# The input projection in a fixed order of instructions, with later places for convolution tiles

## The chip, the cores and the metric

The kernel runs on one core of one Trainium2 chip. The metric is the device time of one execution in microseconds. Three runs of the kernel before took 1119.25, 1124.59 and 1125.08 us, with a median of 1124.59.

The core has TensorE (PE; PEld is its weight load), VectorE (DVE), ScalarE (ACT), GpSimd (POOL) and SyncE (SP), which here issues nearly all DMAs. Each engine works through its own instructions in order and waits on semaphores for the others.

## The reference

The model is a diffusion backbone of two layers, in float32, on 512 latent tokens and 256 context tokens of width 1024. Cut to what the change touches:

```
m = silu(c) @ w_ada + b_ada                # shifts, scales, gates of a layer
h = rms_norm(x + pos, g); h = h * (1 + scale) + shift      # context the same
z = h @ w_in                               # split into u (512), v (512), gate (512)
y_a = S5(u)                                # 32 groups of 16 channels, 64 states, both directions
y_a = gelu(y_a + d_skip * u); y_a = y_a * sigmoid(y_a @ w_glu)
v = v * sigmoid(gate)
v = silu(layer_norm(depthwise_conv31(v)))  # conv branch
x = x + gate_1 * (concat(y_a, v) @ w_out)
```

The context tokens only feed the states that S5 starts from. Behind the mixer come a squared-ReLU MLP of width 4096, the second layer (a pooling mixer and another MLP) and a last RMS norm.

## The kernel before

Activations are held with the features on the 128 partitions: 1024 features are eight blocks of 128, and the tokens run along the free axis. Most matmuls are done in float32 split in two parts, high and low, with three products: high by high, low by high, high by low (`mm3`, `split`).

**Input projection of u.** It runs over the eight feature blocks d (L863 to L887 below). For a block, `u_load` issues the DMAs of the code weights (`wah`, `wraw`) and of the projection weights (`wu`). `u_ada` multiplies the code vector with these weights: 16 small matmuls into `ps_ada`, a copy by ScalarE into `ada`, two selecting matmuls with `sel`, and two small operations of VectorE, which give the block's scale and shift `ab`. `norm_x` adds the position embedding to all eight blocks, squares them on ScalarE (`sx`, `sq`), sums the squares over blocks on VectorE, and sums over partitions on TensorE, by matmuls against a column of ones (`ps_ms`). `bcast_rsqrt` takes the reciprocal root, sets it on a diagonal `dg`, and spreads it to all partitions by one matmul (`ps_r`). `w_step` splits the projection weights into `wuh` and `wul`. `x_step` makes the modulated block (`tn` on VectorE, its high part `nh` on ScalarE, its low part `nl` on VectorE) and runs 12 matmuls of 512 columns into four accumulators `ux`. `c_step` does the same for a context block with 6 matmuls into `uc`. A table, `CORD`, says in which turn each context block is done.

**Discretisation.** `discretise` (called in turn 2), `phases` and `discretise_b` (turn 3) compute the constants of the state-space part from its parameters: many small operations on VectorE, and 32 copies on ScalarE into the tables `PG` and `PO`.

**State-space part.** The 32 groups are done in eight steps of four. `step_params` prepares a step's tables (`gg`, `O`, `hx`, `Bb`; `sd` and from it, by DMA, `Kt`), and `step_main` runs it: `ps_v` from the transposed inputs `U`, the scan on VectorE (`rr`, `tv`), and the output `ps_y`.

**Work handed out between the steps.** The strings `FILL0` (behind the first three `step_params`) and `FILL` (behind each step) say what other work is emitted there: `v` a tile of values and gates (48 matmuls into `ps_vg`), `c` a depthwise convolution of a quarter of the channels (16 DMAs `cvt<-vpad`, 32 matmuls into `ps_cv`), `a` some tiles of the remaining code weights, `y` and `z` the activations of half the outputs, `n` the layer norm of the conv branch, `h` the second load of x, `k` and `g` the gate of y_a, `w` the output projection.

**Order.** The program is written in one stream, and a scheduler that keeps a model of the times sets the order on each engine when the kernel is built. What the strings and `CORD` give is the order in which work is emitted, which the scheduler may change.

Of the kernel before, what the change touches and what calls it, by code (L numbers as in the profile page):

```python
# [8 lines left out]
F32 = mybir.dt.float32  # L9
# [88 lines left out]
def body(tc, I, out, dbg=None):  # L98
    nc = tc.nc
    V, S, G, PE = nc.vector, nc.scalar, nc.gpsimd, nc.tensor  # L100
    dma = nc.sync.dma_start

    def dq(t, i):
        return S.dma_start if t[i % len(t)] == "S" else dma

# [6 lines left out]
    def add(e, o, a, b):  # L112
        e.tensor_tensor(o, a, b, op=OP.add)
# [38 lines left out]
    with tc.tile_pool(name="persist", bufs=1) as P, tc.tile_pool(name="ps", bufs=1, space=PSUM) as PS:  # L152
# [152 lines left out]
        def mixer0(P0):  # L305
# [26 lines left out]
            x0 = htile("x0", [128, KT, L])  # L332
            load_x(x0, "xK")
            ctx = P0.tile([128, KT, LC], F32, name="ctx", tag="A")
# [19 lines left out]
            def ada_pe(srcs, ld, tag="n"):  # L354
                n = len(srcs)
                ws = [l(src) for l, src in zip(ld, srcs)]

                def go():
                    ps = bank("ps_ada", tag)
                    for i, w in enumerate(ws):  # L360
                        for kt in (0, 2, 4, 6, 1, 3, 5, 7):
                            j = kt // 2
                            PE.matmul(ps[32 * j:32 * j + 32, i * 128:i * 128 + 128], S2[:, kt, :], w[kt],  # L363
                                      start=kt % 2 == 0, stop=kt % 2 == 1, tile_position=(0, 32 * j))
                    a = P0.tile([128, 256], F32, name="ada", tag="ada", bufs=1)[:, :n * 128]
                    copy(S, a, ps[:, 0:n * 128])
                    p2 = ps[:, 256:256 + 2 * n]
                    for i in range(n):
                        PE.matmul(p2[:, 2 * i:2 * i + 2], a[:, i * 128:i * 128 + 128], sel[:, 0:2], start=True, stop=True)
                    return p2.rearrange("p (m v) -> p m v", v=2)  # L370
                return go
# [9 lines left out]

            sx = P0.tile([128, 2, L], F32, name="sx", tag="ysb")
            Rs = [small(L), small(LC)]

            def norm_x():
                for d in range(KT):
                    add_pos_k(E("pos", d), x0, d)
                    if d < 2:
                        S.activation(sx[:, d], x0[:, d], AF.Square)
                    else:  # L390
                        q = w4("sq", "cv")
                        S.activation(q, x0[:, d], AF.Square)
                        add(V, sx[:, d % 2], sx[:, d % 2], q)
                add(V, sx[:, 0], sx[:, 0], sx[:, 1])
                copy(S, Rs[0], bcast_rsqrt([sx[:, 0]], L, D))

            def norm_c():
                qs = []
                for d in range(0, KT, 2):
                    q = w4("sq", "cv")  # L400
                    S.activation(q.rearrange("p (a b) -> p a b", a=2), ctx[:, d:d + 2], AF.Square)
                    if qs:
                        add(V, qs[0], qs[0], q)
                    qs.append(q)
                add(V, qs[0][:, 0:LC], qs[0][:, 0:LC], qs[0][:, LC:2 * LC])
                copy(S, Rs[1], bcast_rsqrt([qs[0][:, 0:LC]], LC, D))

# [3 lines left out]
            ux = [bank("ux", "s"), bank("ux", "s"), u2[:, 0], u2[:, 1]]  # L411
            uc = [bank("uc", "c") for _ in range(2)]
            ab = P0.tile([128, KT, 2, 2], F32, name="ab")
# [3 lines left out]
            def u_load(d):  # L417
                adas[d] = ada_pe([I["wada0"][d, 0], I["wada0"][d, 1]], (ada_half, ada_full))
                wus[d] = w4("wu", WU[d % len(WU)])
                dma(wus[d], I["win_u"][d])  # L420
                if d == 0:
                    dma(ctx, I["ctxT"])
                if d == 2:
# [6 lines left out]

            def u_ada(d):
                p2 = adas[d]()
# [4 lines left out]
            whl = {}  # L437

            def u_mod(src, R, n, d, v, oh, ol, el):
                t = tmp("tn", n)  # L440
                stt(t, src, ab[:, d, 1, v:v + 1], R, OP.mult, OP.mult)
                split_shift(oh, ol, t, ab[:, d, 0, v:v + 1])

# [8 lines left out]
            def w_step(d):  # L452
                if d in (0, 1):
                    w = P0.tile([128, 2, GQ, T + 2, PH], F32R, name="wuhl", tag="O", bufs=2).rearrange("p r q t h -> p (r q t h)")
                    whl[d] = w[:, 0:512], w[:, 512:1024]
                else:
                    whl[d] = w4("wuh", "e", F32R), w4("wul", "e", F32R)
                split(*whl[d], wus[d], S, V)

            def x_step(d):  # L460
                u_mod(x0[:, d], Rs[0], L, d, 0, nh[:, d], nl[:, d], E("ul", d))
                u_mm(nh[:, d], nl[:, d], d, ux)

            def c_step(d):
                c2 = w4("c2", "cv", F32R)
                ch, cl = c2[:, 0:LC], c2[:, LC:2 * LC]
                u_mod(ctx[:, d], Rs[1], LC, d, 1, ch, cl, E("ucl", d))
                u_mm(ch, cl, d, uc)

# [108 lines left out]
            def discretise_b(cfr, cfi):  # L578
# [7 lines left out]

                t = gh(w4("tb", "cv")[:, :512])
                cmul(EC("bb"), Bb[:, :, 0], Bb[:, :, 1], gh(Br_), gh(Bi_), bc(cfr), bc(cfi), t)
# [3 lines left out]

            def phases():
                te = small(NG * NB // 2)
                n, lv = 1, 1
                while n < NB:
# [3 lines left out]
                    n *= 2  # L600
                    lv += 1

            def step_params(st):
# [258 lines left out]

            QS = []  # L863
            u_load(0)
            u_ada(0)
            norm_x()
            u_load(1)
            w_step(0)
            x_step(0)
            u_ada(1)  # L870
            norm_c()
            cf = None
            for d in range(1, KT):
                if d + 1 < KT:
                    u_load(d + 1)
                if 1 < d < KT:
                    u_ada(d)
                w_step(d)
                for i in CORD[d]:
                    c_step(i)  # L880
                if d < KT:
                    x_step(d)
                if d == 2:
                    cf = discretise()
                if d == 3:
                    phases()
                    discretise_b(*cf)  # L887
            Z = P0.tile([96, NG, T, PH], F32, name="Z", tag="A")
# [31 lines left out]
            def ada_rest(m, d):  # L920
                p2 = ada_pe([I["wada0b"][m - 2, d], I["wada0b"][m - 2, d + 1]], (ada_full, ada_full), AT)()
                add(V, mod[:, 0, m, d:d + 2], p2[:, :, 0], bada[:, 0, m * KT + d:m * KT + d + 2])
# [346 lines left out]
```

## Time and profile before

| What | Value |
|---|---|
| Runs | 1119.25, 1124.59, 1125.08 us; median 1124.59 |
| Profiled execution | 1127.26 us, its span 1125.1 us |
| TensorE busy | 1045.0 us (93% of the span) |
| VectorE busy | 810.7 us (72%) |
| ScalarE busy | 514.6 us (46%) |
| GpSimd busy | 23.8 us (2%) |
| Mean granted clock of TensorE | 0.969 |

The span is the time from the first to the last instruction of the profiled execution; about 2 us of the time lie around it. Busy time is the time in which an engine has an instruction in hand. The profile counts a float32 matmul as two instructions. "x4 [0.85 <-DVE sx L113]" in a row means that four instructions stand together, and that the engine was idle for 0.85 us before them until VectorE had written `sx` in line 113. An f32 matmul instruction ends by the model of the profile, and records of successive ones overlap; the distance of their starts is the time that one takes.

### The profile page before, as it was taken

Reading aid. Unit: us, or ns where it says so; the run is one execution under the profiler, and the core shown is the slowest. Engines: PE = TensorE matmul, PEld = TensorE weight load, DVE = VectorE, ACT = ScalarE, POOL = GpSimd, SP = SyncE. Lnnn points to the kernel's source line nnn. Section 1 sums busy time; section 2 is a strip of 40 time slices with the busy share of each in tenths; the row PEclk is TensorE's granted clock in tenths of the full one; section 3 lists DMA queues with packets and bytes.
Section 4 is the critical chain, followed back from the end, with each engine's and each line's share of the span. In section 5 each row is a group of like instructions: output and inputs, shape, how many; then the busy total and the mean of one; then the engine's idle time right before and its main releaser. Section 6 shows DMA issues by size and latency. Waiting matters only on the chain.

```text
span 1125.1 us, 18913 instructions
## 1 busy us (share of the span) xinstructions
PE 1045.0 (93%) x7342; PEld 892.9 (79%) x7342; DVE 810.7 (72%) x1511; ACT 514.6 (46%) x910; POOL 23.8 (2%) x44
## 2 busy tenths in 40 slices
PE   3879998985998999999999999989989999999996
PEld 2657665544788988888789999989989988888896
DVE  7965699778688989868746679899866553343365
ACT  4365544454755643313325456566545332133253
POOL 0002000000000000000000000000000000000000
PEclk9999899997899999999999999999989999999998
DMA  9430634145546788878745555545535522233252
GB/s 348 146 128 30 184 85 148 44 123 187 160 137 208 208 281 290 304 230 282 242 149 170 182 174 186 162 133 177 160 121 181 178 94 94 95 108 97 94 169 94
DMA packets 63594, 185.09 MB, mean 165 GB/s; under 512 B 8464, under 2 KB 14608, under 8 KB 63376
## 3 DMA queue, kind: packets, MB, share of 16 engines
q1 hardware_dynamic: 63504, 183.87, 50.6%
q8 instruction: 58, 0.95, 0.3%
q14 instruction: 32, 0.26, 0.1%
HBM read 175.22 MB, written 2.10 MB: 158 GB/s over the span
## 4 chain that ended last, share of the span: by engine, by line
PE 53%; DMA 8%; DVE 6%; ACT 1%; issue 1%; POOLq 0%; POOL 0%; DVEq 0%; ACTq 0%
PE ps L150 17%; PE ps L149 17%; PE ps L148 17%; DMA wraw<-in_wadaT 5%; DMA wraw<-in_w 3%; DVE junk L1000 2%; DVE wlo L116 2%; ACT whi L139 1%; PE ps_o L148 0%; PE ps_r L194 0%; DVE tn L125 0%; PE ps_o L150 0%; PE ps_o L149 0%; PE ps_p L150 0%; PE ps_p L148 0%
## 5 line engine op out<-in xcount | busy, mean ns | idle before, releaser
L139 ACT ACTIVATE whi<-wraw 128x1024 fp32r<-128x1024 f32 (+1 forms) x232 | 231.7, 1000 | 397.2 <-PE ps L149 268.9
L116 DVE TENSOR_TENSOR wlo<-wraw,whi 128x1024 fp32r<-128x1024 f32 (+1 forms) x232 | 266.3, 1149 | 107.4 <-ACT whi L139 104.5
L148 PE MATMUL ps<-nh,whi 128*128 128x256 f32 (+3 forms) x768 | 245.8, 322 | 4.4 <-ACT nh L285 2.5
L150 PE MATMUL ps<-nh,wlo 128*128 128x256 f32 (+3 forms) x768 | 246.4, 322 | 1.8 <-DVE wlo L116 1.7
L149 PE MATMUL ps<-nl,whi 128*128 128x256 f32 (+3 forms) x768 | 246.7, 322 | 1.2 <-DVE nl L125 1.2
L148 PE MATMUL ps<-hh,whi 128*128 128x512 f32 (+3 forms) x768 | 244.3, 318 | 0.0
L150 PE MATMUL ps<-hh,wlo 128*128 128x512 f32 (+3 forms) x768 | 243.7, 317 | 0.1
L149 PE MATMUL ps<-hl,whi 128*128 128x512 f32 (+3 forms) x768 | 243.4, 317 | 0.0
L148 PEld LDWEIGHTS ps<-nh,whi 128*128 128x128 f32 x768 | 148.0, 194 | 15.7 <-ACT nh L285 3.7
L150 PEld LDWEIGHTS ps<-nh,wlo 128*128 128x128 f32 x768 | 148.0, 193 | 13.2 <-DVE wlo L116 3.1
L149 PEld LDWEIGHTS ps<-nl,whi 128*128 128x128 f32 x768 | 148.1, 193 | 11.8 <-DVE nl L125 1.7
L150 PEld LDWEIGHTS ps<-hh,wlo 128*128 128x128 f32 x768 | 144.2, 188 | 12.0 <-DVE wlo L116 0.9
L149 PEld LDWEIGHTS ps<-hl,whi 128*128 128x128 f32 x768 | 144.3, 188 | 10.6
L148 PEld LDWEIGHTS ps<-hh,whi 128*128 128x128 f32 x768 | 144.5, 188 | 9.9
L125 DVE SCALAR_TENSOR_TENSOR h<-ps,mod,h 128x512 f32<-128x512 f32 (+3 forms) x96 | 54.9, 571 | 85.9 <-PE ps L150 85.9
L1000 DVE SCALAR_TENSOR_TENSOR junk<-wraw,csil 128x1024 f32<-128x1024 f32 x56 | 68.3, 1220 | 19.9 <-DMA wraw<-in_wadaT 19.6
L116 DVE TENSOR_TENSOR hl<-rl,hh 128x256 fp32r<-128x256 f32 (+3 forms) x96 | 48.5, 511 | 4.8 <-ACT hh L139 3.7
L1026 ACT ACTIVATE rl<-ps 128x256 f32<-128x256 f32 (+3 forms) x96 | 41.9, 437 | 5.7 <-PE ps L150 4.6
L148 PE MATMUL ps_o<-nh,whi 128*128 128x256 f32 x128 | 38.2, 299 | 3.6 <-ACT whi L139 3.0
L150 PE MATMUL ps_o<-nh,wlo 128*128 128x256 f32 x128 | 37.2, 295 | 1.8 <-DVE wlo L116 1.8
L149 PE MATMUL ps_o<-nl,whi 128*128 128x256 f32 x128 | 36.8, 288 | 0.1
L363 PE MATMUL ps_ada<-wraw,S 128*32 128x128 f32 x512 | 25.7, 311 | 9.4 <-DMA wraw<-in_wada0b 8.5
(266 smaller groups left out, 1371.1 us busy)
## 6 DMA issues: line engine op xcount, KB each, us to landing
wraw<-in_w SPq DMA_DIRECT2D x192, 512.0 KB, 3.5
wraw<-in_wadaT SPq DMA_DIRECT2D x56, 512.0 KB, 4.6
wraw<-in_wada0b SPq DMA_DIRECT2D x24, 512.0 KB, 4.4
wraw<-in_wout SPq DMA_DIRECT2D x32, 256.0 KB, 2.6
cvt<-vpad SPq DMA_DIRECT2D x64, 67.5 KB, 2.0
wah<-in_wada SPq DMA_DIRECT2D x16, 256.0 KB, 3.8
wraw<-in_wada SPq DMA_DIRECT2D x8, 512.0 KB, 8.1
wraw<-in_win_vg SPq DMA_DIRECT2D x8, 512.0 KB, 4.2
```

What stands on the lines that cost most here:

```text
L116: e.tensor_tensor(o, a, b, op=OP.subtract)
L125: V.scalar_tensor_tensor(o, a, s, b, op0=op0, op1=op1)
L139: S.activation(o, a, AF.Copy)
L148: PE.matmul(ps, wh, xh, start=first, stop=False)
L149: PE.matmul(ps, wh, xl, start=False, stop=False)
L150: PE.matmul(ps, wl, xh, start=False, stop=last)
L363: PE.matmul(ps[32 * j:32 * j + 32, i * 128:i * 128 + 128], S2[:, kt, :], w[kt], start=kt % 2 == 0, stop=kt % 2 == 1, tile_position=(0, 32 ...
L1000: V.scalar_tensor_tensor(junk, w, 1.0, csil, op0=OP.mult, op1=OP.mult, accum_out=r)
L1026: S.activation(t, ps, AF.Relu)
```

## The change

In the projection stage the orders of VectorE, ScalarE and TensorE are now those of the code. The operations of the discretisation are recorded (`held`) and emitted by `drain(n)` in portions that a table gives (`UD`). The sums of squares no longer pass through VectorE: each block's squares go to TensorE, which adds over blocks in `ps_ms`. The code weights' matmuls (`adas[d]`) are parted from the selection (`pick`) and done one or two blocks ahead. Context blocks have two tables, one for the modulation (`CPREP`) and one for the matmuls (`CMM`). The split projection weights get other buffers (`WH`). The loads of x and of the context stand elsewhere in the order of the DMA queue. In `FILL0` and `FILL`, the first value tile and one portion of code weights move behind the first step, the convolutions and the code weights `a2` one to three places later.

```
-FILL0 = ("v0 a3", "", "")
-FILL = ("v1", "", "c0 v2 a2", "c1 c2 v3", "a3 y", "c3", "h k a4 n", "w7 z", "g w9 w9")
+UD = (14, 0, 34, 4, 15)
+WH = "OOeeyOOe"
+CPREP = ((), (), (0, 1), (2,), (3,), (4, 5), (6, 7), ())
+CMM = ((), (), (), (0, 1), (2,), (3,), (4, 5), (6, 7))
+FILL0 = ('', '', '')
+FILL = ('v0 a3 v1', 'c0 v2', 'a2', 'c1 v3', 'a3 y', 'c2 c3', 'h k a4 n', 'w7 z', 'g w9 w9')
...
-            sx = P0.tile([128, 2, L], F32, name="sx", tag="ysb")
...
-                add(V, sx[:, 0], sx[:, 0], sx[:, 1])
-                copy(S, Rs[0], bcast_rsqrt([sx[:, 0]], L, D))
...
+            def sums(v, q, n, d):
+                for j in range(n // 128):
+                    PE.matmul(pms[v][:, j:j + 1], q[:, 128 * j:128 * j + 128], ones[:, 0:1], start=d == j == 0, stop=d == KT - 1 and j == n // 128 - 1)
...
+            with tc.manual_schedule(engines=UENG):
+                held.append([])
+                phases(discretise())
+                todo = held.pop()
...
+                load_x(x0, "xK")
+                u_load(0)
+                u_load(1)
+                dma(ctx, I["ctxT"])
+                drain(UD[0])
+                for d in range(KT):
+                    norm_x(d)
+                    drain(UD[1])
+                adas[0] = adas[0]()
...
+                low(scaled([x_job(0, rms(0, L, between))]))
+                adas[1] = adas[1]()
+                u_load(2)
+                w_step(1)
+                for d in range(0, KT, 2):
+                    norm_c(d)
+                u_mm(nh[:, 0], nl[:, 0], 0, ux)
+                u_ab(1)
+                low(scaled([x_job(1, Rs[0])]))
+                adas[2] = adas[2]()
+                u_load(3)
+                sums_c()
+                u_ab(2)
+                w_step(2)
+                drain(UD[2])
+                for d in range(1, KT):
+                    if d + 2 < KT:
+                        adas[d + 2] = adas[d + 2]()
...
+                    u_mm(nh[:, d], nl[:, d], d, ux)
+                    r = scaled([x_job(i, Rs[0]) for i in (d + 1,) if i < KT] + [c_job(i) for i in CPREP[d]])
+                    if d == 1:
+                        rms(1, LC, lambda: drain(UD[3]))
+                    low(r)
+                    if d + 2 < KT:
+                        u_ab(d + 2)
...
+                    if d + 2 < KT:
+                        w_step(d + 2)
+                    drain(UD[4])
+                drain(len(todo))
```

Three places show how it changes the orders. The first is the start of TensorE's program. Before, one sum of `sx` stands behind the first block's code weights:

```order
L363 MATMUL ps_ada<-wah,S_87 32x128 x8
L363 MATMUL ps_ada<-wraw,S_87 32x128 x8
L369 MATMUL ps_ada<-sel,ada 128x2 x2
L187 MATMUL ps_ms<-ones,sx 128x1 x4
L363 MATMUL ps_ada<-wah,S_87 32x128 x8
L363 MATMUL ps_ada<-wraw,S_87 32x128 x8
L194 MATMUL ps_r<-dg,ones 128x512
```

After, on the same engine at the same place:

```order
L406 MATMUL ps_ms<-ones,sq 128x1 x32
L378 MATMUL ps_ada<-wah,S_87 32x128 x8
L378 MATMUL ps_ada<-wraw,S_87 32x128 x8
L386 MATMUL ps_ada<-sel,ada 128x2 x2
L433 MATMUL ps_r<-dg,ones 128x512
L378 MATMUL ps_ada<-wah,S_87 32x128 x8
L378 MATMUL ps_ada<-wraw,S_87 32x128 x8
L470 MATMUL ux<-wuhl,nh 128x512
```

The sums have become 32 matmuls and stand ahead of the first code weights.

The second place is on ScalarE, in the later blocks of the projection. Before (`nh` is the high part of a block of x and each numbered `c` that of a context block):

```order
L285 ACTIVATE nh<-tn,ab 128x512
L570 ACTIVATE PG<-scr 64x8x32 x4
L570 ACTIVATE PO<-scr 64x8x32 x4
L285 ACTIVATE c_613<-tn,ab 128x256
L139 ACTIVATE O<-Cc 64x8x16 x2
L285 ACTIVATE c_624<-tn,ab 128x256
```

After, where the second `nh` is that of the last block:

```order
L491 ACTIVATE nh<-tn,ab 128x512
L491 ACTIVATE c_727<-tn,ab 128x256
L491 ACTIVATE c_728<-tn,ab 128x256
L155 ACTIVATE wuh<-wu 128x512
L114 ACTIVATE PG<-scr 64x8x32 x8
L114 ACTIVATE PO<-scr 64x8x32 x5
L491 ACTIVATE nh<-tn,ab 128x512
```

Before, the copies into PG and PO stand in groups of eight between the blocks; after, 13 stand together ahead of the last block's `nh`.

The third place is on TensorE around step 5 of the state-space part. Before, where `ps_cv` is the third convolution (`c2`):

```order
L788 MATMUL ps_cv<-cvt,hx 32x512 x2
L666 MATMUL ps_k<-hx,Bb 16x128 x5
L634 MATMUL ps_g<-ident,gg 128x128 x4
L666 MATMUL ps_k<-hx,Bb 16x128 x3
L788 MATMUL ps_cv<-cvt,hx 32x512 x19
L666 MATMUL ps_k<-hx,Bb 16x128 x8
L788 MATMUL ps_cv<-cvt,hx 32x512 x8
L724 MATMUL ps_y<-Kt,U 64x128 x2
```

After, where the first row is the last `ps_v` of step 5:

```order
L734 MATMUL ps_v<-U,GT 64x96
L386 MATMUL ps_ada<-sel,ada 128x2 x2
L709 MATMUL ps_k<-hx,Bb 16x128 x16
L378 MATMUL ps_ada<-wraw,S_87 32x128 x16
L831 MATMUL ps_cv<-cvt,hx 32x512 x16
L386 MATMUL ps_ada<-sel,ada 128x2 x2
L831 MATMUL ps_cv<-cvt,hx 32x512 x8
L767 MATMUL ps_y<-Kt,U 64x128 x2
```

This convolution stood ahead of the `ps_v` of step 5 before, and stands behind it after.

## Rows read from the trace of the kernel before

**Rows 1.** Windows, by stage: stretch, length, busy by engine (x instructions), clock, DMA share, GB/s.

```profile
0.00:27.75 27.75, 10.13 (x82) 7.06 (x82) 21.38 (x71) 10.99 (x20) 2.71 (x13) 1.00 0.95 347
27.75:44.19 16.44, 14.46 (x102) 9.86 (x102) 14.39 (x82) 5.22 (x11) 0.74 (x1) 1.00 0.47 159
44.19:96.70 52.51, 41.72 (x266) 31.06 (x266) 40.62 (x88) 29.84 (x57) 5.68 (x2) 0.90 0.33 110
96.70:123.00 26.30, 23.55 (x211) 17.82 (x209) 5.17 (x6) 13.80 (x35) 0.47 (x5) 0.89 0.36 109
...
204.00:232.00 28.00, 27.58 (x302) 15.98 (x300) 17.47 (x31) 14.87 (x42) 0.06 (x1) 1.00 0.28 78
232.00:271.70 39.70, 27.14 (x296) 14.42 (x294) 37.49 (x61) 20.52 (x48) 2.07 (x3) 0.90 0.48 151
271.70:294.80 23.10, 20.39 (x184) 14.87 (x185) 14.47 (x27) 14.58 (x27) 1.01 (x1) 0.72 0.58 182
```

**Rows 2.** Timeline of TensorE, first 38 us: start, length, instruction, idle time before.

```profile
18.57 1.01 PE L369 MATMUL ps_ada<-sel,ada 128*128 128x2 f32 x4 [2.85 <-ACT ada L139]
20.43 1.87 PE L187 MATMUL ps_ms<-ones,sx 128*128 128x1 f32 x8 [0.85 <-DVE sx L113]
22.23 1.08 PE L363 MATMUL ps_ada<-wah,S 128*32 128x128 f32 x16
...
25.04 2.05 PE L194 MATMUL ps_r<-dg,ones 128*128 128x512 f32 x2 [0.88 <-DVE dg L110]
...
29.91 0.63 PE L449 MATMUL ux<-wuhl,nh 128*128 128x512 f32 x1
30.33 0.63 PE L448 MATMUL ux<-wuhl,nh 128*128 128x512 f32 x1
...
37.41 0.39 PE L449 MATMUL ux<-wuhl,nh 128*128 128x512 f32 x1
37.64 0.40 PE L448 MATMUL ux<-wuhl,nh 128*128 128x512 f32 x1
```

**Rows 3.** Timeline, VectorE and ScalarE, first squares.

```profile
8.37 1.29 DVE L113 TENSOR_TENSOR x<-x,sm 128x512 f32<-128x512 f32 x2 [2.41 <-DMA x<-in_xK]
...
9.10 1.23 ACT L389 ACTIVATE sx<-x 128x512 f32<-128x512 f32 x2 [4.98 <-DVE x L113]
```

**Rows 4.** Chain of waits at 367 us: start, length, piece.

```profile
367.37 0.34 PE ps_ms L187 x4
```

**Rows 5.** Lines of VectorE before 27.75 us: count, busy, mean ns, idle before.

```profile
L113 DVE TENSOR_TENSOR x<-x,sm 128x512 f32<-128x512 f32 x8 | 6.7, 884 | 2.4 <-DMA x<-in_xK 2.4
```

**Rows 6.** Timeline of VectorE, 27 to 45 us.

```profile
27.75 0.75 DVE L125 SCALAR_TENSOR_TENSOR tn<-x,ab,scr 128x512 f32<-128x512 f32 x1
...
34.46 0.63 DVE L125 SCALAR_TENSOR_TENSOR scr<-scr 128x64 f32<-128x64 f32 x4
...
44.19 0.74 DVE L125 SCALAR_TENSOR_TENSOR tn<-x,ab,scr 128x512 f32<-128x512 f32 x1
```

**Rows 7.** Timeline of VectorE at step 5.

```profile
232.17 0.96 DVE L110 TENSOR_TENSOR rr<-ps_v,E 128x768 f32<-128x768 f32 x1 [2.69 <-PE ps_v L691]
233.05 0.95 DVE L110 TENSOR_TENSOR tv<-ps_v,E 128x768 f32<-128x768 f32 x1
```

**Rows 8.** Lines of VectorE, 44.19 to 96.7 us, by form.

```profile
L125 DVE SCALAR_TENSOR_TENSOR c<-tn,ab,c 128x256 fp32r<-128x256 f32 x8 | 3.8, 479 | 0.0
...
L116 DVE TENSOR_TENSOR wul<-wu,wuh 128x512 fp32r<-128x512 f32 x4 | 2.8, 688 | 5.3 <-ACT wuh L139 2.7 <-issue 2.6
```

**Rows 9.** Timeline of ScalarE, 53 us.

```profile
53.50 2.48 ACT L570 ACTIVATE PG<-scr 64x256 f32<-64x256 f32 x4 [0.93 <-DVE scr L116]
```

**Rows 10.** Timeline of the DMA queue of SyncE, 275 us.

```profile
275.27 5.07 SPq L678 DMA_DIRECT2D Kt<-sd  x8
```

**Rows 11.** Timeline of TensorE, conv norm.

```profile
277.51 1.67 PE L187 MATMUL ps_ms<-ones,ln 128*128 128x1 f32 x8 [1.02 <-DVE ln L113]
...
281.63 2.06 PE L194 MATMUL ps_r<-dg,ones 128*128 128x512 f32 x2
```

More of the change, by code (lines that the diff above doesn't have):

```diff
@@ L367, in go, with pick @@
                     p2 = ps[:, 256:256 + 2 * n]
-                    for i in range(n):
-                        PE.matmul(p2[:, 2 * i:2 * i + 2], a[:, i * 128:i * 128 + 128], sel[:, 0:2], start=True, stop=True)
-                    return p2.rearrange("p (m v) -> p m v", v=2)
+                    def pick():
+                        for i in range(n):
+                            PE.matmul(p2[:, 2 * i:2 * i + 2], a[:, i * 128:i * 128 + 128], sel[:, 0:2], start=True, stop=True)
+                        return p2.rearrange("p (m v) -> p m v", v=2)
+                    return pick
                 return go
@@ L397, in norm_c @@
[L397 to L406, printed above, removed]
+            pms = bank("ps_ms", "m"), bank("ps_ms", "c")
@@ new lines, in sums, with norm_x, norm_c @@
+            def sums(v, q, n, d):
+                for j in range(n // 128):
+                    PE.matmul(pms[v][:, j:j + 1], q[:, 128 * j:128 * j + 128], ones[:, 0:1], start=d == j == 0, stop=d == KT - 1 and j == n // 128 - 1)
+            def norm_x(d):
+                add_pos_k(E("pos", d), x0, d)
+                q = w4("sq", "cv")
+                S.activation(q, x0[:, d], AF.Square)
+                sums(0, q, L, d)
+            csq = []
+            def norm_c(d):
+                q = tmp("sqc")
+                S.activation(q.rearrange("p (a b) -> p a b", a=2), ctx[:, d:d + 2], AF.Square)
+                csq.append(q)
@@ new lines, in sums_c, with rms @@
+            def sums_c():
+                for d in range(KT):
+                    sums(1, csq[d // 2][:, d % 2 * LC:], LC, d)
+            def rms(v, n, between):
+                nj = n // 128
+                y = rsqrt_small(pms[v][:, :nj], 128, nj, 1.0 / D)
+                between()
+                dg = tmp("dg")[:, 0:n]
+                mul(V, dg.rearrange("p (a b) -> p a b", a=nj), ident[:, None, :].to_broadcast([128, nj, 128]),
+                    y[:, :, None].to_broadcast([128, nj, 128]))
+                pr = bank("ps_r", "mc"[v])
+                PE.matmul(pr[:, :n], ones, dg, start=True, stop=True)
+                copy(S, Rs[v], pr[:, :n])
+                return pr[:, :n]
@@ L411, in mixer0 @@
             ux = [bank("ux", "s"), bank("ux", "s"), u2[:, 0], u2[:, 1]]
-            uc = [bank("uc", "c") for _ in range(2)]
+            uc = []
             ab = P0.tile([128, KT, 2, 2], F32, name="ab")
@@ L429, in u_load, with u_ab @@
                     dma(dsk, I["dsk"])
[L431 removed]
+            def u_ab(d):
                 p2 = adas[d]()
@@ L585, in gh @@
                     return t.rearrange("p (s q h) -> p s q h", q=GQ, h=PH)
-                t = gh(w4("tb", "cv")[:, :512])
+                t = gh(small(512))
                 cmul(EC("bb"), Bb[:, :, 0], Bb[:, :, 1], gh(Br_), gh(Bi_), bc(cfr), bc(cfi), t)
@@ L601, in phases @@
                     lv += 1
+                discretise_b(*cf)
             def step_params(st):
```

109 lines of the change are left out of this document (54 added, 55 removed).

## The prediction, made before the changed kernel ran

> **What bounds the kernel now.** I read the windows view first, by stage [rows 1]: the input projection ends at 96.7 us, the first step of the state-space part starts at 123, and the output projection starts at 294.8. From there on TensorE is fed by weights that no part of the change touches, so the later 830 us of the span stand, and all that can be won or lost lies in the first 295 us. There no engine is full. Up to 27.75 us VectorE waits for sums, reciprocals and code weights in turn, and TensorE is busy for 10.1 us. In 44.19 to 96.7 TensorE (41.7 of 52.5 us), VectorE (40.6) and ScalarE (29.8) hand work to one another. In 96.7 to 123 VectorE has nearly nothing to do (5.2 of 26.3), in 204 to 232 TensorE is full (27.6 of 28) while VectorE, which paces the steps, idles for 10.5. In 232 to 271.7 it is the other way round. So I then read the timelines of TensorE and VectorE at the edges of these stretches.
>
> **The change part by part.** It does four things.
>
> *1. Sums of squares on TensorE.* Before, VectorE adds up squares and TensorE takes one 4-matmul sum (1.87 us at 20.43, ending at 22.3) [rows 2]. Now every block's square goes to TensorE: 32 matmuls for x, 16 for the context, and 11 additions of VectorE go. The first square is ready at 9.10 + 0.62 = 9.7 us [rows 3]. One block's sum is the 1.87 us row, so 8 blocks are 15.0 us and the sums end at 9.7 + 15.0 = 24.7, against 22.3. That is the price at TensorE's lower level. The windows row names a granted clock of 1.00 here, but 512-column matmuls stand 0.42 us apart at 30 us and 0.23 us apart at 37.4 [rows 2], so the engine ran at 1.2 GHz until after 30 us and at 2.4 later; I go by the spacing. The bound from below is the same sum later in the kernel, 0.34 us for a block [rows 4]: then the eight position additions set the end (8.37 + 6.7 = 15.1 [rows 3, 5], one square and one block's sum behind: 16.5). I take 24.7, since the nearest rows in time have the low clock.
>
> The Trainium skill, "TensorE: Matmul & The Clock Gate", its part on the HAM clock gate, says that the array starts at 1.2 GHz and goes to 2.4 after sustained work. The trace does not bear that out soon: between 20.43 and 30.8 TensorE has little idle time and is at 1.2 GHz all along. By that rule the sums would end near 20, not 24.7. That is a rival below.
>
> *2. From the sums to the first modulated block.* Before: 22.3 to 27.75 [rows 6], 5.45 us. Now the code weights of block 0 stand behind the sums in TensorE's fixed order: 2 × 0.96 us (16 code matmuls, 22.23 row), the copy on ScalarE 0.4, two selecting matmuls 0.9 (18.57 row, less the overlap of records), the two small operations for `ab` 0.3, the split of the weights 0.6, the diagonal 0.6, and the broadcast 2.05 (25.04 row) [rows 2]. Some of it overlaps with the reciprocal on VectorE; I sum 7.2. The first block then starts at 24.7 + 7.2 = 31.9, 4.2 late. To block 2: code weights of block 1 1.9, the 12 matmuls of block 0 at 0.42 = 5.1, selection 0.5, code weights of block 2 0.9, the 16 code matmuls of the context's sums 2.7 (32 passes of 0.085; at the low clock 7.5), selection 0.5, `ab` and weights 0.9, and 34 handed-out operations that VectorE has to do ahead of it, 34 × 0.13 = 4.4 (0.63 us for four, records overlapping [rows 6]). That is 17 after block 0, so block 2 starts at 48.9, where it starts at 44.19 now: 4.7 late.
>
> *3. The loop over the other blocks.* Before, 44.19 to 96.7, 52.5 us. It has holes because the scheduler mixes in the discretisation of the state-space part where it liked. In the changed order VectorE's work in the loop can be added up. Records of neighbouring operations overlap by 0.08 us (0.96 us recorded, the next 0.88 later [rows 7]), so I take 0.66 for a 0.75 operation. Six blocks of x: 2 × 0.66 = 7.9. Five of weights: 0.60 each by [rows 8], with `ab` 0.27: 4.4. Six hand-outs of 15 operations at some 0.12: 10.8. Eight context blocks, two operations of 0.40 each: 6.3 [rows 8]. Two splits of the next weights 2.3, the context's reciprocal 1.6, waiting for those weights 1.5. Sum 34.8. New is a wait: ScalarE has 13 copies into PG and PO ahead of the last block's `nh` in its fixed order, and four such took 2.48 us together at 53.50 [rows 9], 0.61 each: 13 × 0.61 = 7.9, beside some 2 us of other work of VectorE: +6. Behind it are the last 12 matmuls, 2.8 us, and one stretch at the low clock, 1.5: 45.1 us in all. The projection then ends at 48.9 + 45 = 93.9, some 3 us earlier. Bounds: 84 (without the copies and at the full clock from the start) and 99 (two low-clock stretches, no overlap at `nh`).
> The gap to the first step, 26.3 us, I leave: the 48 matmuls of the first value and gate tile still stand right there, though the table has them later, and what VectorE was relieved of in the loop (some 16 us) fits into its 21 idle us [rows 1].
>
> *4. The conv branch.* In 204 to 232 VectorE waits 10.5 us while TensorE runs the last value and gate tile and the third convolution; `rr` of step 5 starts at 232.17 after waiting for its `ps_v` [rows 7]. In the new order that convolution stands behind step 5's `ps_v`, and beside VectorE's full stretch (37.5 of 39.7 us [rows 1]), where TensorE has 12.6 us free. The most to be had is 10.5, the worst is that the same matmuls delay step 6 (some 4 us). I take 6, since half of the idle time belongs to the value tile, which has not gone anywhere.
> At the end of the conv branch the last `ps_y` is put ahead of the norm's sum and six code-weight tiles instead of four stand ahead of `ps_r`. `ps_y` waits for its table, whose eight transfers are issued from 275.27 to 280.34 [rows 10]. So the sum, at 277.51 now [rows 11], starts at least 2.8 us later, with a landing some 3.3; the `ps_y` work that stood behind `ps_r` at 281.63 and is now done ahead of it takes back 1.3: +2, bounds 0 (the table comes earlier with the rest) and +6 (all of `ps_y` and both tiles stand in the way).
>
> Sum, in the profile's own time: −3 − 6 + 2 = −7. From 1127.3 that is 1120.3. The profiled execution lies 2.7 above the median of the runs, 1124.6, so the forecast is 1117.6.
>
> **The rivals.**
> R1, the clock rises during the sums. If it does after five of the eight blocks, the sums end at 9.7 + 5 × 1.87 + 3 × 0.34 = 20.1, 4.6 earlier; block 0's 12 matmuls take 2.8 instead of 5.1, and `ps_r` with two tiles of code weights, at half their time, give another 1.8. In all 8.7 less, so about 1109 (1104 to 1113). For it: the sums are 15 us of matmuls without a gap. Against it: the row at 30 us above.
> R2, spreading the convolution frees nothing: the matmuls are the same and TensorE was 27.6 of 28 us busy there [rows 1]; VectorE's wait moves one step on. Then −3 + 2 remains, 1123.6 (1119 to 1129). For it: of all that the table hands out later, the first value tile has not moved in TensorE's order. Against it: the 12.6 us of free TensorE time in the stretch behind.
> R3, the slower one: in the fixed order TensorE has a gap in every block (it waits for `nl`, then for `ab`, and VectorE has 15 other operations ahead of it), and it goes back to 1.2 GHz in the loop. A block is then 12 × 0.42 + 1.9 + 0.9 = 7.9 us, and 2.5 for a context block, against some 6 by VectorE: about +4.9 for a block. It decides from three of the seven blocks on; with four it is 1117.6 + 19.6 = 1137 (1130 to 1150). For it: the loop before shows a mean granted clock of 0.90 with gaps of 3 us [rows 1]. Against it: these gaps have cost it one block in six or so.
> The page named above says that idle stretches drop the clock again, which speaks for R3.
>
> **How the numbers follow.** Chances: forecast 0.45 (own range 1111 to 1124), R1 0.20, R2 0.20, R3 0.15. A measurement of this kernel can't tell less than 0.5% (5.6 us) from no change. Faster, under 1119.0: nearly all of R1 (0.19), 0.32 of the forecast's 0.45, and little of R2: 0.52. Slower, over 1130.2: R3 and a tail of the others, 0.16. The rest, 0.32, is no change. Range: 1106 to 1128 leaves out R1's lower end, R3 and the forecast's tails, about 2 in 10.
>
> **What would show it.** Right if the sums on TensorE take 15 us and end near 25, block 2's `tn` starts near 49, `nh` of the last block waits behind the PG and PO copies, the projection ends near 94, and VectorE's idle time in step 5 falls by about 6. Wrong if 512-column matmuls stand 0.42 apart in three or more blocks of the loop (R3), if they stand 0.23 apart before 32 us (R1), or if the state-space part, from its first `ps_v` to the output projection, takes as long as its 172 us now (R2).

## The result: about 1% slower

The changed kernel took 1133.8 us (median of four runs, 1128.68 to 1142.66) against 1123.9 for the kernel before on the same chip: ratio 1.0105, interval 1.0067 to 1.0143. Two later measurements gave 1.0121 (1.0098 to 1.0144) and 1.0110 (1.0079 to 1.0140). The forecast was 1117.6, and the range ended at 1128. The direction was wrong.

Three traces of the changed kernel and two of the one before agree on where it falls back:

| | before | changed |
|---|---|---|
| last matmul of the projection ends | 96.7, 95.0 | 100.3, 100.4, 101.2 |
| first `rr` of the state-space part | 128.3, 125.8 | 131.1, 131.1, 133.0 |
| last step's `rr` of `ps_v` | 258.7, 259.5 | 250.2, 249.2, 253.5 |
| `ps_mu` of the conv norm | 265.5, 266.3 | 270.1, 269.1, 273.3 |
| output projection starts | 294.8, 294.8 | 297.9, 299.3, 304.4 |
| first MLP matmul | 360.5, 360.5 | 365.7, 366.9, 373.5 |

So 5 to 13 us are lost by the start of the MLP, where the forecast had 7 won. The rest of the program is the same work and takes 761.2 to 766.8 us in these five traces: the first trace of the changed kernel (1128.68 us) is its fastest execution, and both of before (1127.3 and 1127.9) lie 4 to 5 us above that kernel's median of 1122.8 over 89 executions (one of 1473.0 us is left out, as is one of 2028.7 of e_pair below).

### The profile page after: what moved, and what is told of

Same layout as the page of the kernel before. It is cut to its first block, busy times and chain, and to the rows that moved or that the text cites. A ratio compares the mean times of both kernels' runs of the same rounds, so it can differ in the third digit from the quotient of the medians.

```text
span 1126.9 us, 19060 instructions
## 1 busy us (share of the span) xinstructions
PE 1047.1 (93%) x7426; PEld 906.7 (80%) x7426; DVE 810.1 (72%) x1500; ACT 515.0 (46%) x910; POOL 21.6 (2%) x44
## 4 chain that ended last, share of the span: by engine, by line
PE 52%; DMA 8%; DVE 6%; ACT 1%; issue 1%; POOLq 0%; POOL 0%; DVEq 0%; ACTq 0%
PE ps L166 17%; PE ps L165 17%; PE ps L164 17%; DMA wraw<-in_wadaT 4%; DMA wraw<-in_w 3%; DVE wlo L132 2%; DVE junk L1079 2%; ACT whi L155 1%; DVE tn L141 1%; PE ps_p L166 0%; PE ps_p L164 0%; PE ps_p L165 0%; PE ps_r L210 0%; DVE h L141 0%; DVE hl L132 0%
## 5 line engine op out<-in xcount | busy, mean ns | idle before, releaser
L282 ACT ACTIVATE sq<-h 128x256 f32<-128x256 f32 (+2 forms) x64 | 24.8, 407 | 17.2 <-DVE h L141 16.0
```

The costliest lines, as they stand in the source:

```text
L282: S.activation(q, h[:, d, tk], AF.Square)
```

## The profile after

The windows of the changed kernel, cut where its own stages end: first `tn`, `tn` of block 2, end of the projection, first `ps_v`; then from the first `rr` to `ps_mu`, and from there to the output projection (columns as in [rows 1]):

```profile
0.00:30.12 30.12, 19.37 (x118) 17.22 (x122) 11.12 (x29) 8.01 (x13) 2.32 (x13) 1.00 0.85 309
30.12:50.73 20.61, 17.35 (x152) 14.16 (x144) 11.58 (x45) 6.33 (x12) 0.00 (x0) 0.83 0.54 179
50.73:100.27 49.54, 41.16 (x270) 32.27 (x271) 38.82 (x132) 26.85 (x50) 4.96 (x5) 0.86 0.31 102
100.27:125.22 24.95, 21.78 (x209) 16.91 (x207) 18.76 (x30) 18.00 (x46) 0.16 (x2) 0.93 0.38 118
131.09:270.09 139.00, 118.02 (x1258) 75.05 (x1258) 131.07 (x203) 69.84 (x169) 5.70 (x13) 0.97 0.41 123
270.09:297.88 27.79, 19.62 (x209) 13.93 (x207) 13.19 (x29) 16.45 (x31) 1.01 (x1) 0.87 0.50 159
```

The kernel before, first `rr` to `ps_mu`, and `ps_mu` to the output projection:

```profile
128.27:265.50 137.23, 122.85 (x1253) 75.29 (x1251) 123.12 (x193) 68.12 (x166) 4.86 (x13) 0.97 0.39 111
265.50:294.82 29.32, 23.43 (x204) 15.87 (x203) 20.57 (x39) 16.72 (x32) 1.01 (x1) 0.73 0.63 210
```

Behind the length stand TensorE, its weight load, VectorE, ScalarE and GpSimd. In the state-space stretch VectorE idles 139.00 − 131.07 = 7.9 us after and 137.23 − 123.12 = 14.1 before: 6.2 less, near the forecast's 6. That the two agree is luck: the forecast meant the wait at step 5, and there the idle time between the `rr` of step 4 and that of step 5 fell by 11, from 11.2 us to 0.2, while 5 us came up elsewhere. From the first `rr` to the last step's it takes 119.1 us after and 130.4 before, but from there to `ps_mu` 19.9 us after and 6.8 before, so the stretch is not shorter. VectorE does 8 us more there, and 7 less in the tail (13.19 instead of 20.57), and the tail is as long as before, since it is a chain of waits and not a lot of work.

The start on TensorE, against [rows 2]:

```profile
8.37 13.78 PE L406 MATMUL ps_ms<-ones,sq 128*128 128x1 f32 x64 [8.37 <-ACT sq L411]
22.08 1.08 PE L378 MATMUL ps_ada<-wah,S 128*32 128x128 f32 x16
...
27.41 2.05 PE L433 MATMUL ps_r<-dg,ones 128*128 128x512 f32 x2 [1.87 <-DVE dg L126]
```

The sums end at 22.1, where the one sum of before ended at 22.3. What is new is that the code weights of block 0 come behind them, so that `ps_r` starts 2.4 us later than at 25.04.

VectorE ahead of block 2, against [rows 6] (four pieces of one hand-out, and the `tn` behind it):

```profile
43.18 0.18 DVE L114 SCALAR_TENSOR_TENSOR scr<-scr 128x32 f32<-128x32 f32 x1
...
45.27 1.52 DVE L114 SCALAR_TENSOR_TENSOR scr<-scr 128x64 f32<-128x64 f32 x6
...
48.58 0.74 DVE L114 SCALAR_TENSOR_TENSOR scr<-scr 128x64 f32<-128x64 f32 x3
...
50.07 0.74 DVE L114 SCALAR_TENSOR_TENSOR scr<-scr 128x64 f32<-128x64 f32 x3
50.73 0.74 DVE L141 SCALAR_TENSOR_TENSOR tn<-x,ab,scr 128x512 f32<-128x512 f32 x1
```

The 34 operations take from 43.18 to 50.73, 7.55 us, 0.22 each, where I had 0.13.

ScalarE in the loop, waits in brackets, and with it VectorE's wait for the last block:

```profile
69.57 1.06 ACT L155 ACTIVATE whi<-wraw 128x1024 fp32r<-128x1024 f32 x1 [3.55 <-DMA wraw<-in_win_vg]
...
75.51 1.06 ACT L155 ACTIVATE whi<-wraw 128x1024 fp32r<-128x1024 f32 x1 [4.09 <-DMA wraw<-in_win_vg]
76.47 0.71 ACT L491 ACTIVATE nh<-tn,ab 128x512 fp32r<-128x512 f32 x1
...
85.33 4.76 ACT L114 ACTIVATE PG<-scr 64x256 f32<-64x256 f32 x8
90.10 3.04 ACT L114 ACTIVATE PO<-scr 64x256 f32<-64x256 f32 x5
93.17 0.72 ACT L491 ACTIVATE nh<-tn,ab 128x512 fp32r<-128x512 f32 x1
```

```profile
70.66 1.22 DVE L132 TENSOR_TENSOR wlo<-wraw,whi 128x1024 fp32r<-128x1024 f32 x1 [3.52 <-ACT whi L155]
...
76.59 1.23 DVE L132 TENSOR_TENSOR wlo<-wraw,whi 128x1024 fp32r<-128x1024 f32 x1 [0.58 <-ACT whi L155]
...
93.92 0.75 DVE L141 SCALAR_TENSOR_TENSOR nl<-tn,ab,nh 128x512 fp32r<-128x512 f32 x1 [3.67 <-ACT nh L491]
```

Both splits of the first value tile's weights (`whi`) stand ahead of the `nh` of block 5 (76.47) and wait for their transfers. On VectorE `wlo` waits for `whi`, and block 5's `tn` (74.88) stands behind the first of these waits: they cost VectorE 3.52 and 0.58 us. The 13 copies into PG and PO do hold the last block, as forecast.

TensorE in the loop, behind two of its holes, and at its end:

```profile
52.84 0.70 PE L433 MATMUL ps_r<-dg,ones 128*128 128x256 f32 x2 [4.44 <-DVE dg L126]
...
56.30 0.80 PE L470 MATMUL ux<-wuh,nh 128*128 128x512 f32 x1
56.89 0.63 PE L471 MATMUL ux<-wul,nh 128*128 128x512 f32 x1
57.32 0.63 PE L472 MATMUL ux<-wuh,nl 128*128 128x512 f32 x1
57.75 0.63 PE L470 MATMUL ux<-wuh,nh 128*128 128x512 f32 x1
...
79.00 1.08 PE L378 MATMUL ps_ada<-wah,S 128*32 128x128 f32 x16 [4.16 <-DVE ab L129]
...
94.34 0.50 PE L470 MATMUL uc<-wuhl,c 128*128 128x512 f32 x1 [1.56 <-ACT c L491]
...
97.55 0.39 PE L470 MATMUL ux<-wuh,nh 128*128 128x512 f32 x1
```

Behind the hole of 4.44 us block 2's matmuls stand 0.43 apart, the 1.2 GHz level, for nine of twelve; behind that of 4.16 us block 5's do for seven. The window row shows a granted clock of 0.86 for this stretch, and 0.90 for the loop of before [rows 1]. Low stretches are not new: in the first trace of before 17 of the loop's matmuls start 0.43 behind the one ahead, in three groups (from 46.3, 69.7 and 83.2 us), here 15. At the end 12 context matmuls (94.34 to 97.55) stand ahead of the last block's.

The tail, against [rows 11]:

```profile
267.34 0.69 PE L767 MATMUL ps_y<-Kt,U 128*64 128x128 f32 x4 [8.38 <-DMA Kt<-sd]
...
279.06 0.70 PE L767 MATMUL ps_y<-Kt,U 128*64 128x128 f32 x4 [3.27 <-DMA Kt<-sd]
...
281.82 1.18 PE L203 MATMUL ps_ms<-ones,ln 128*128 128x1 f32 x8
...
286.08 1.12 PE L210 MATMUL ps_r<-dg,ones 128*128 128x512 f32 x2
```

`ps_mu` (270.09) stands behind one `ps_y` that waits for `Kt`, the sum behind another. VectorE reaches the last step's `rr` 8.5 us earlier, but the `sd` from which the first of these `Kt` is made 4.2 us later: six of the eight additions of the second load of x now stand in between (the changed kernel first; before, two came ahead of `ps_mu` and six after it):

```profile
255.47 2.48 DVE L129 TENSOR_TENSOR h<-h,sm 128x512 f32<-128x512 f32 x4
...
258.75 1.27 DVE L129 TENSOR_TENSOR h<-h,sm 128x512 f32<-128x512 f32 x2
260.05 0.21 DVE L129 TENSOR_TENSOR sd<-sd 16x64 f32<-16x64 f32 x1
260.30 1.29 DVE L129 TENSOR_TENSOR h<-h,sm 128x512 f32<-128x512 f32 x2
```

The same `sd` in the kernel before:

```profile
255.88 0.21 DVE L113 TENSOR_TENSOR sd<-sd 16x64 f32<-16x64 f32 x1
```

## The experiments

Two theories at first: P, the fixed order of the projection costs the time; H, the later hand-out does. Beside them C, the time is TensorE's low clock, against W, it is waits. Ratios are to the kernel before on the same chip. The last four columns are from one trace each.

| run | ratio (interval) | projection ends | first `rr` | `ps_mu` | first MLP matmul |
|---|---|---|---|---|---|
| after_again | 1.0121 (1.0098–1.0144) | 100.4 | 131.1 | 269.1 | 366.9 |
| e_proj | 1.0198 (1.0171–1.0225) | 100.1 | 130.8 | 274.4 | 377.3 |
| e_fill | 1.0020 (1.0007–1.0034) | 95.5 | 124.5 | 262.8 | 353.1 |
| e_ud13 | 1.0094 (1.0064–1.0124) | 100.0 | 133.7 | 271.4 | 365.9 |
| e_whi | 1.0029 (1.0008–1.0051) | 97.0 | 126.8 | 266.5 | 358.0 |
| e_early | 1.0043 (1.0020–1.0067) | 99.0 | 128.2 | 269.0 | 359.8 |
| e_pair | 1.0079 (1.0051–1.0107) | 99.6 | 130.8 | 271.9 | 365.3 |
| after_third | 1.0110 (1.0079–1.0140) | 101.2 | 133.0 | 273.3 | 373.5 |
| e_warm | 1.0070 (1.0043–1.0097) | 103.1 | 131.8 | 274.7 | 362.9 |
| e_comb | 1.0053 (1.0030–1.0075) | 91.5 | 128.0 | 266.8 | 359.8 |
| e_combw | 1.0037 (1.0016–1.0058) | 97.7 | 129.9 | 268.7 | 359.0 |
| e_aftera | 1.0102 (1.0063–1.0141) | 98.9 | 136.1 | 276.5 | 366.2 |
| e_comba | 1.0062 (1.0042–1.0083) | 90.0 | 132.9 | 263.9 | 360.3 |
| e_befa | 1.0068 (1.0039–1.0098) | 95.0 | 127.9 | 274.9 | 366.8 |
| e_combv | 1.0078 (1.0054–1.0101) | 90.5 | 133.8 | 269.2 | 359.1 |
| e_combv2 | 1.0030 (1.0010–1.0051) | 91.9 | 129.2 | 265.1 | 356.4 |

Two cautions for all of them. Outside the projection the scheduler sets the orders again for each kernel, so an edit also moves instructions far behind it. And a column of one trace says where a stage ends, not what it costs: eight of the edited kernels reach the first MLP matmul ahead of both traces of the kernel before (360.5), e_fill by 7 us, and each is slower by its ratio; what follows that matmul takes 761 to 771 us in these traces.

**The two parts apart.**

```
e_proj:  changed kernel, but  FILL0 = ("v0 a3", "", "");  FILL = ("v1", "", "c0 v2 a2", "c1 c2 v3", "a3 y", "c3", ...)
e_fill:  kernel before, but   FILL0 = ('', '', '');  FILL = ('v0 a3 v1', 'c0 v2', 'a2', 'c1 v3', 'a3 y', 'c2 c3', ...)
```

> The fixed order of the projection alone: the changed kernel with the hand-out strings of the kernel before. Theory P (the projection stage costs the time: its end was at 100.3 us in the changed kernel's trace and at 96.7 before, with TensorE at the low clock in three blocks): 6 to 14 us slower than the kernel before. Rival H (the later hand-out costs it: the conv norm's sum starts at 281.8 instead of 277.5): within 4 us of the kernel before.

> The hand-out strings alone: the kernel before with the strings of the changed one. Theory P: within 4 us of the kernel before, or faster. Rival H: 6 to 14 us slower than the kernel before, with the last ps_y and the norm's sum late again.

The fixed order alone costs 2.0%, 23 us, more than P allowed; the hand-out alone costs 0.2%. Together they cost 1.2%. By these two runs the projection's order is what costs, and the later hand-out takes back some 9 us of it, but only there: with the old strings the steps, whose first `rr` is 3 to 5 us late, fall behind to 274.4 at `ps_mu` and 309.3 at the output projection. Why they fall behind is not shown. A rival stays open: that any new order of what stands behind the projection costs. e_befa below leaves the projection as it was (95.0) and still reaches the output projection only at 306.5.

**More executions of both.**

> The changed kernel once more, unchanged, for more executions and a second trace. Theory C (clock): all of the difference between executions and between the two kernels is time at the low clock. In the four executions so far, span times (1 minus mean granted clock) is 38.3, 43.1, 51.3 and 43.0 us, and the span less that is 1088.6, 1090.0, 1089.6 and 1088.0; C expects 1087 to 1091 for that remainder in every execution, of both kernels, and a median time of 1130 to 1136. Rival W (waits): the remainder itself is larger than in the kernel before by 5 us or more, since engines wait for one another for longer, and does not stay within 4 us.

> The kernel before once more, for a second trace of it: its first profiled execution (1127.3 us) is slower than 18 of the others (median 1121.8). Theory C (clock): span times (1 minus mean granted clock) is 29 to 35 us in it, the projection ends again at 95 to 98 us, and the output projection starts at 290 to 295. Rival: the stages of the mixer are just as in the first trace and the difference lies behind them.

before_again: 1127.9 us, projection end 95.0, output projection at 294.8. Its clock term came out at 38.3, above the 29 to 35 expected. The remainder (span times mean granted clock) over all executions has a median of 1089.7 in the changed kernel (14) and 1086.5 in the one before (89), with single ones between 1078 and 1095; the clock term 42.4 against 34.7. So neither theory holds as it was put: 7.7 us of the difference go with the low clock and 3.2 do not, and the remainder is not constant. This parts the difference and does not name its cause: the low clock can be what waits leave behind.

**Single losses of the projection.**

```
e_whi    + in the loop, behind low(r) of the last block (d == KT - 2):
         +     pre.extend(ring.get(I["win_vg"][m], [KT, 128], el=E("wv", m)) for m in range(2))
         - vgt(0):  ring.get(...)      + vgt(0):  pre[m]
e_early  - UD = (14, 0, 34, 4, 15)     + UD = (14, 2, 18, 4, 15)
         - sums_c(); u_ab(2); w_step(2); drain(UD[2])
         + sums_c(); drain(UD[2]); u_ab(2); w_step(2)
e_ud13   - UD = (14, 0, 34, 4, 15)     + UD = (14, 0, 34, 4, 13)
e_pair   - sums(0, q, L, d)
         + psq.append(q) if d is even, else add(V, q, q, psq[-1]) and sums(0, q, L, d, 1)
```

> The changed kernel with the splits of the first value tile's weights (whi on ScalarE, wlo on VectorE) put behind the last block's nh, in the fixed order; in the changed kernel they stood ahead of two blocks' nh and waited 3.55 and 4.09 us for their transfers. If that wait is what the loop lost, the projection ends 5 to 7 us earlier, near 94, and the time falls by 4 to 7 us. Rival: the loop is paced by VectorE's other work and by TensorE's low clock, and the first value tile starts later instead: projection less than 3 us earlier, time within 2 us of the changed kernel.

> The changed kernel with the 34 operations that VectorE did ahead of block 2 (43.2 to 50.7 us) moved: 16 between the position additions, 18 ahead of the selection of block 2, where VectorE waited 3.8 us. If these operations and the hole of 4.4 us that they make on TensorE, with the low clock behind it, are what the start of the loop lost, block 2's tn starts at 45 to 47 us instead of 50.7, the projection ends 4 to 6 us earlier and the time falls by 3 to 6 us. Rival (the wait for whi at 69 to 76 us takes it up, since it waits for a transfer): tn earlier, projection end within 2 us, time within 2 us.

> The changed kernel with hand-outs of 13 instead of 15 operations a block (UD ends in 13), so that 3 instead of 13 of the PG and PO copies stand ahead of the last block's nh on ScalarE. If these copies cost what the trace shows (VectorE waits 3.67 us for nh), the projection ends 3 to 4 us earlier, near 97, and the time falls by 2 to 4 us against the changed kernel. Rival: the copies are only moved behind nh, and Z or the first step's tables are late by as much: within 1 us of the changed kernel.

> The changed kernel with the squares of two blocks added on VectorE, so that TensorE takes 16 instead of 32 sums for x. At the low clock these sums were 13.8 us, from 8.4 to 22.1. If TensorE's sums set the start, they end at 17 to 18, the first ux matmul starts 4 to 5 us earlier (near 27), the projection ends 3 to 5 us earlier, the time falls by as much. Rival (TensorE's low clock without a long stretch of work, or block 2's operations, take it up): projection end within 2 us.

e_whi gives back 9 us of time, more than expected, and 3 to 4 us at the end of the projection, less than expected: block 5's `tn` starts at 71.59 instead of 74.88, close to VectorE's first wait for `whi`, 3.52 us, and not to ScalarE's two together. e_early moves block 2's `tn` by 7 us:

```profile
43.76 0.74 DVE L141 SCALAR_TENSOR_TENSOR tn<-x,ab,scr 128x512 f32<-128x512 f32 x1
```

and the end of the projection by only 1 to 2: there its rival was right. Block 5's `tn` starts at 74.89, as in the changed kernel, since VectorE now waits 4.25 and 2.40 us for `whi`. The time falls by 8 us all the same, and with it the first MLP matmul by 6 to 7 us (more against the third trace). How much of these two gains is the removed wait, and how much the scheduler's other order behind it, the runs do not part. e_ud13 did not end the projection earlier in its trace, and its 0.0027 lie within the intervals. The wait for the copies is gone there and the last block's `nl` starts 2 us earlier, but it takes 2.40 us instead of 0.75, beside the second of two multiplications of GpSimd, and ends at 94.37 where it ended at 94.67:

```profile
89.72 4.09 POOL L126 TENSOR_TENSOR hx<-sm,sel 128x1024 f32<-128x1024 f32 x2 [36.08 <-DVE tn L141]
...
91.97 2.40 DVE L141 SCALAR_TENSOR_TENSOR nl<-tn,ab,nh 128x512 fp32r<-128x512 f32 x1
```

e_pair missed: its sums end at 22.5, as before, since VectorE now waits for each pair's second square ahead of the next position addition. It says nothing on the price of the sums.

**The clock.**

```
e_warm   + spare = rms(0, L, between)
         + behind u_mm of d in (1, 4):   12 times PE.matmul(spare, whl[d][0][:, 0:128], nh[:, d], start=True, stop=True)
```

> The changed kernel, unchanged, beside the three below on the same chip and for a third trace. 0.9 to 1.3% slower than the kernel before; projection end at 100 to 101 us, first MLP matmul at 365 to 368 us (360.5 in both traces of before). Rival: the stages shift by several us from trace to trace, and the two traces of it so far are not typical.

> The changed kernel with 12 matmuls more of 512 columns, into a spare accumulator that nothing reads, behind block 1 and behind block 4 on TensorE, in the holes of 4.4 and 4.2 us (all it adds is work). Theory C (clock): the low clock behind these holes is the cost; with the holes filled, blocks 2 and 5 run at 0.23 us a matmul, and the projection ends 2 to 4 us earlier than in the changed kernel. Rival W (VectorE paces the loop, TensorE's clock only fills time that it would wait): the matmuls are faster but the projection ends within 1 us of the changed kernel's, since the next block waits for VectorE.

after_third ends the projection at 101.2 and reaches the first MLP matmul at 373.5, later than expected: as its rival says, the stages shift by several us from trace to trace. In e_warm, with 12 matmuls in the hole, block 2 runs at 0.23 us a matmul, but starts when it did, and the next block waits instead:

```profile
49.93 2.88 PE L957 MATMUL ps_r<-nh,wuhl 128*128 128x512 f32 x12
53.85 0.70 PE L433 MATMUL ps_r<-dg,ones 128*128 128x256 f32 x2 [1.03 <-DVE dg L126]
...
56.15 0.50 PE L470 MATMUL ux<-wuh,nh 128*128 128x512 f32 x1
56.49 0.40 PE L471 MATMUL ux<-wul,nh 128*128 128x512 f32 x1
...
62.34 0.69 PE L378 MATMUL ps_ada<-wah,S 128*32 128x128 f32 x16 [2.81 <-DVE ab L129]
...
95.04 0.80 PE L470 MATMUL uc<-wuhl,c 128*128 128x512 f32 x1 [3.78 <-ACT c L491]
95.63 0.63 PE L471 MATMUL uc<-wuhl,c 128*128 128x512 f32 x1
96.06 0.63 PE L472 MATMUL uc<-wuhl,c 128*128 128x512 f32 x1
```

VectorE's last `nl` starts at 94.62, not earlier than in the three traces without these matmuls (93.92, 94.05, 94.80): in the loop the clock follows from VectorE's pace and does not set it, which is rival W. The projection ends later, at 103.1, outside W's 1 us: the low clock now stands behind the last hole, where nothing waits for VectorE any more, and 11 matmuls 0.43 apart cost some 2 us there. That the whole run is 0.4% nearer to the kernel before is at the limit of the two intervals.

**The repairs together.**

e_comb is e_whi, e_early and e_ud13 in one; e_combw adds e_warm's matmuls.

> The changed kernel with three edits together: the value tile's weight splits behind the last block (as e_whi), the 34 operations moved into VectorE's waits (as e_early), and hand-outs of 13 (as e_ud13). If the three losses are separate (about 9, 8 and 3 us by ratios 1.0029, 1.0043 and 1.0094 against 1.0121), the sum takes the kernel below the one before: 1% faster, projection end at 89 to 92 us. Rival: they are the same time counted thrice, with the end set by the transfers and by the steps behind: projection end at 95 to 97 us, time within 0.4% of the kernel before.

> e_comb with the 24 unread matmuls of e_warm. Theory C: 1 to 3 us faster than e_comb, as blocks 2 and 5 run at the full clock. Rival W: the same within 1 us, or slower by up to 5 us where the holes are gone and the extra matmuls (24 times 0.23 us) stand in the way.

The projection of e_comb ends at 91.5, 9 us earlier than the changed kernel's, as the additive theory had it; the time falls by 6 us, not by 20. The windows of e_comb, projection and the gap to the first `rr`:

```profile
31.80:91.50 59.70, 54.29 (x398) 44.01 (x398) 46.09 (x151) 27.02 (x52) 4.95 (x5) 0.89 0.43 140
91.50:128.00 36.50, 30.69 (x262) 23.50 (x261) 25.21 (x44) 26.47 (x62) 0.00 (x0) 0.80 0.33 105
```

The gap takes up 5 of the 9 us. In e_combw the projection ends 6 us later (24 × 0.23 = 5.5) and the time is no worse: the end of the projection no longer decides.

**What holds the first step.** Ahead of step 0's `ps_g` and `ps_v` e_comb has code-weight tiles on TensorE. Four runs shift the hand-out:

```
e_aftera (on the changed kernel), e_comba (on e_comb):  FILL = ('v0 v1', 'c0 v2 a1', 'a2', 'c1 v3 a1', 'a4 y', ...)
e_befa (on the kernel before):  FILL0 = ("v0", "", "");  FILL = ("v1", "a1", "c0 v2 a2", "c1 c2 v3 a1", "a4 y", ...)
e_combv (on e_comb):   FILL = ('v0 a1', 'c0 v1 a2', 'v2 a2', 'c1 v3', 'a3 y', ...)
e_combv2 (on e_comb):  FILL = ('v0 a2', 'c0 v1 a1', 'v2', 'c1 v3 a2', 'a3 y', ...)
```

> The changed kernel with the first portion of code weights (a3) handed out later, one tile each behind steps 1 and 3 and four behind step 4. Theory G (the gap between the projection and the first step is set by the code-weight tiles that stand ahead of step 0's ps_g and ps_v and by their transfers, not by the projection): the first rr comes 3 to 8 us earlier than the 131 to 133 us of the changed kernel, and the time falls by 2 to 6 us. Rival V (the second value tile, 48 matmuls, moves into their place and takes as long): first rr within 2 us, time within 3 us or slower, since the code weights then lie in the later steps.

> The same hand-out on e_comb, whose projection ends at 91.5 us but whose first rr is at 128.0, a gap of 36.5 us. Theory G: the gap falls to 28 or less, the first rr comes at 118 to 122, and the time falls 4 to 8 us under e_comb's, to the kernel before or below it. Rival V: first rr at 126 to 130 and no gain.

> The same on the kernel before. Theory G: first rr 3 to 6 us earlier than the 125.8 and 128.3 of its two traces, time 0 to 0.4% faster. Rival V: no gain or slower.

> e_comb with one tile of code weights instead of three ahead of the first step (two behind step 1), and the second value tile behind step 1. Theory F (the first step waits for whatever is handed out ahead of it: code weights and their transfers in e_comb, a second value tile in e_comba): first rr at 118 to 122 us against 128.0, and the time 3 to 7 us under e_comb's (ratio 0.998 to 1.002). Rival D (the first step waits for its own tables, which VectorE and ScalarE finish at 123 us): first rr at 126 to 128, time within 2 us of e_comb.

> The same with two tiles of code weights ahead of the first step and one behind step 1. Theory F: between e_comb and e_combv, first rr at 122 to 126. Rival D: 126 to 128.

Theory G falls: in all three the first `rr` comes later or no earlier. Theory F's numbers fall too, and D's: 133.8 and 129.2. In e_combv VectorE waits for the second half of `ps_g`, which stands behind value-tile matmuls that the scheduler has put between the halves:

```profile
125.76 1.22 DVE L126 TENSOR_TENSOR tg<-PG,Bb 128x1024 f32<-128x1024 f32 x1 [8.13 <-PE ps_g L678]
```

TensorE then runs 15 more value-tile matmuls ahead of the rest of `ps_v` (132.53), and `rr` follows at 133.84. So something else steps into the place each time. What the first step would need is its own work ahead of all of it on TensorE, and the strings do not say that. It wasn't tried, and how much it would give stays open. No version beat the kernel before; the nearest are e_fill, e_whi and e_combv2.

## Why the prediction was wrong, by its steps

1. *Sums on TensorE:* right in kind. 13.8 us from 8.4, end at 22.1 instead of 24.7; rows at 1.2 GHz to 32.7 us, so not R1.
2. *To block 2:* first `tn` at 30.1 (31.9 forecast), so 8.0 us behind the sums where 7.2 were booked (the terms listed add up to 6.8). Block 2 at 50.7 (48.9). The term that was mis-sized most is the 34 handed-out operations: 7.5 us instead of 4.4. I had taken 0.13 from a row in which the scheduler of before had mixed independent operations [rows 6]; in code order they stand 0.22 apart. The context's sums took 4.4 instead of 2.7.
3. *The loop:* this step failed. 45 forecast, 49.5 measured (50.73 to 100.27), and its sign with it: 3.6 us later instead of 3 earlier. VectorE's own work was summed about right. Up to the last `nl` it waited for some 9.4 us where 7.5 were booked: 4.1 for `whi` where 1.5 were booked for weights, 3.7 for the copies, not 6, and 1.6 for selections and `nh`, which had been put at nothing. Behind the start of the last `nl` come 6.4 us, not 4.3: the 12 context matmuls ahead of the last block's, 3.2 us, were left out. The first four hand-outs of 15 took 10.0 us together instead of 7.2 (the first 3.0, from `scr` at 55.15 to `tn` at 58.15), but the fifth 0.3 instead of 1.8, since 13 of its operations are the copies on ScalarE. In time the fixed order cost far more than the loop's 3.6 us: e_proj is 23 slower, and most of that comes up behind the projection. How, stays open.
4. *The conv branch:* this step failed too. The wait at step 5 went, 11 us of it, and the last `rr` came 8.5 us earlier. But I booked VectorE's idle time as time won and put at nothing what `ps_mu` waits for: the `sd` and the `Kt` made from it stood behind additions and splits that had come later before, and `ps_mu` came 4 us later. In e_fill, with the old projection, the `Kt` wait ahead of `ps_mu` is 8.42 us as well, and the hand-out alone is at +0.2%, not −4 us: R2's outcome, by another mechanism (the wait did not move on a step). The prediction's own sign for R2 came true: from the first `ps_v` to the output projection it took 172.7, 173.0 and 177.4 us, against 171.9.
5. *The tail:* +2 forecast. From `ps_mu` on it took 27.8, 30.2 and 31.1 us, 29.3 and 28.5 before: nothing clear. The sum itself starts 4.3 later, since `ps_mu` does (4.6).
6. *The gap of 26.3:* held (25.0). From the output projection to the first MLP matmul it took 67.6 to 69.1 us, 65.7 before; the prediction had left this stretch as it was.

R3, the slower rival, had the sign and holes with the low clock behind them (nine matmuls of block 2, seven of block 5). But the loop of before had them too (17 matmuls 0.43 apart against 15), and R3's price was the clock: e_warm shows that within the loop the clock is not the price.

## What to carry to other kernels

An idle engine in a trace is not time to be won: ask which instruction on the path to the end would start earlier, and what the scheduler will put into the hole instead. When a scheduled stretch is put into a fixed order, small operations that read each other's results stand further apart than mixed ones (here 0.26 us against 0.14), and an instruction that waits for a transfer holds all that stand behind it on its engine, and what waits for those on other engines; both have to be counted from rows of dependent instructions. When three repairs of one stage do not add up, look at what stands between that stage and the next.

## What was not expected of the hardware

Six VectorE operations of 128x64 in the order of the code, where each reads the one before, took 1.52 us, their starts 0.26 apart, and three 0.74; four of the same shape, mixed from independent chains, took 0.63, their starts 0.14 apart [rows 6]. In every trace one VectorE operation beside GpSimd's multiplications into `hx` is stretched: a `tn` of a context block takes 2.14 us instead of 0.47 in all traces of the changed kernel, an `nl` 2.40 instead of 0.75 in both of the one before. Why is not shown. The time of one execution of the changed kernel on the same chip varied by up to 14 us (1128.68 to 1142.66), and its mean granted clock from 0.966 to 0.955 with it: span times (1 minus clock) went from 38.3 to 51.3 us, and the remainder stayed at 1088.6 and 1089.6 in these two.
